# Attention in a two-layer backbone step: TensorE's program order pinned, modulation weights a page at a time, rows of maxima on SP's queue

## The chip, the cores and the metric

The kernel runs on one core of a Trainium2 chip. It is one launch that reads its inputs from the chip's memory and writes all outputs there. The metric is the device time of one execution in microseconds, the median of several. The engines in the profile are TensorE (PE, with its weight load PEld), VectorE (DVE), ScalarE (ACT), GpSimd (POOL) and SyncE (SP), and 16 DMA engines. DMAs are issued from two queues here: SP's (q1 in the profile) and ACT's (q10).

## The reference

Two layers over 128 context tokens and 1024 latent tokens, width 1024. In each layer a modulated norm feeds one input projection whose columns go to four groups: differential attention, multi-head latent attention (mla), grouped-query attention (gqa) and a Fourier mix. Their outputs go through one output projection, and an MLP follows. What matters here is the attention, which every head computes as

```python
def one_block(qb):
    logits = jnp.concatenate([jnp.einsum("bqhd,bkhd->bhqk", q_i, k_i)
                              for q_i, k_i in zip(qb, keys)], axis=-1) * scale
    probs = jax.nn.softmax(logits, axis=-1)
    ...   # out = sum over parts of einsum("bhqk,bkhd->bqhd", probs, v_i)
```

over the latent keys, the context keys and the cache of 128 past positions, and the modulation, which both token kinds take from

```python
mods = jax.nn.silu(c) @ w + b      # w is ada_w: (1024, 6 * 1024) for each layer
```

There are 16 softmax maps in a layer: eight for the four differential heads, four gqa, four mla.

## The kernel before

Everything is computed with channels or positions in the 128 partitions. Operands of matrix products are split into a high and a low half where the precision asks for it. In the code a layer goes through the norm and the input projection, then `attention`, then the output projection and the MLP. Pages of 4 KB in each partition (`pg` in the profile) are handed out and given back by the kernel itself: `t` takes one, `free` returns it, and a load into a page waits until the last user of that page is done.

`attention` runs over the 16 maps i of a layer (0 to 7 differential, one pass of scores each; 8 to 11 gqa, two passes; 12 to 15 mla, three passes). For map i it interleaves four generators with `run`, which always steps the one that is furthest behind its share:

- `stav(Ms[i])`: scores and products with V of map i, in ten pieces of up to 1024 columns. Scores go into `psB` (TensorE), ACT takes exp from it (L1340) and copies it to 16 bits (L1347), POOL subtracts to get the low half (`sub`, L287), and then TensorE multiplies both halves with V into `psC`. Between a piece's scores and its products with V lie `LAG` pieces, which `pend` holds and `settle` lets go.
- `beside(i)`: first `begin` issues the loads of map i+2 (`stack_diff`, `stack_gqa`, `stack_mla`: queries `qr` and `qp`, keys `kk`). For differential and mla maps `kk` is a tile of 97 rows by 1152 columns, loaded from `sk` or `mk` in one DMA. Then it takes `smax` of map i+1 to its end and some steps (`SMX`) of map i+2. `smax` computes the maxima of each query's scores ahead of the map: products into `psA`, `reduce_max` on DVE (L1297, L1302) into `mx` and `mm`, a small product that turns the nine columns into rows, a scaling into `mr` (L1311), and two DMAs of 4.0 and 4.5 KB that write `mr` into one more row of the query tiles `qr` and `qp` of that map, from where the score products subtract them. At step `LATE` the second and third parts of gqa and mla maps are loaded.
- `mods(MODS[l][i])`: steps of `mod_tiles`, the modulation. One tile has four pages of `ada_w` (`in_ada_p`, 512 KB each, loaded by `mod_stage`), eight products with `csil` (`mod_mm`), a copy on ACT (`acopy`, L290) and four small products with `quads`.
- `values(VM[i])`: V of the mla maps.

Deferred steps (`defer`, `tick`) finish a map: `epi_norm` and its like on DVE, a transposition on TensorE (L1441), and a store of the result to `y_dram` on ACT's queue.

The order in which an engine runs its instructions is not the order of the code. Before, a scheduler chooses among the instructions of all generators by priority (`pri`, `SC_PRI`), and the DMAs on SP's queue are put in an order by it too. An engine runs its own list strictly in order, and so does a queue: an instruction that waits holds everything behind it. A DMA signals its completion on one of eight semaphores that are taken in turn, so an issue may also wait for an older DMA that used the same one.

Lines of the profile: L271 is a DMA issued on SP (`dma`), L275 one on ACT (`dma2`), L278 a product on TensorE (`mm`), L287 a subtraction (`sub`), L290 a copy on ACT (`acopy`).

Of the kernel before, what the change touches and what calls it, by code (L numbers as in the profile page):

```python
# [52 lines left out]
MODS = ((0, 2, 2, 2, 2, 2, 2, 2, 2, 2, 2, 2, 2, 2, 2, 2), (0, 2, 2, 2, 2, 2, 2, 2, 2, 2, 0, 0, 0, 0, 0, 0))  # L53
# [11 lines left out]
LAG = (5, 5, 5)  # L65
LATE = 7
# [4 lines left out]
YO_PRI, RE_PRI, SC_PRI = 40, 60, (60, 0, 0)  # L71
# [129 lines left out]
class Kern:  # L201
    def __init__(self, ctx, tc, I, O):
        self.tc, self.nc, self.I, self.O = tc, tc.nc, I, O
        self.const = ctx.enter_context(tc.tile_pool(name="const", bufs=1))
        sl = ctx.enter_context(tc.tile_pool(name="slots", bufs=1))
        self.small = ctx.enter_context(tc.tile_pool(name="small", bufs=4))
        self.psA = ctx.enter_context(tc.tile_pool(name="psA", bufs=2, space=PSUM))
        self.phase = ctx.enter_context(ExitStack())
        self.split_now = None
        dram = ctx.enter_context(tc.tile_pool(name="dram", bufs=1, space=DRAM))  # L210
        self.sb = Arena(sl, NPG)
        self.x_dram = dram.tile([D, NT], F32, name="x_dram")
        self.y_dram = dram.tile([KT, 128, NT], F32, name="y_dram")
        self.spill(dram)
        self.n = 0
        self.cnt = 0
        self.nx = 0
        self.todo = deque()
        self.pend = deque()
        self.late = []  # L220
        self.ready = set()
        self.ylast = {}
        self.acc = {}
        self.wqk = []

# [51 lines left out]
    def mm(self, out, lhsT, rhs, start, stop, skip=False):  # L277
        self.nc.tensor.matmul(out, lhsT=lhsT, rhs=rhs, start=start, stop=stop, skip_group_check=skip)  # L278
# [144 lines left out]
    def mod_tiles(self, l, js):  # L423

        todo = [(j, half) for j in js for half in range(2)]
        w = self.mod_stage(l, *todo[0])
        yield
        for i, (j, half) in enumerate(todo):
# [4 lines left out]
            if i + 1 < len(todo):  # L433
                w = self.mod_stage(l, *todo[i + 1])
# [11 lines left out]
            yield  # L446

# [5 lines left out]
    def mod_stage(self, l, j, half):  # L453
        return [self.stage(self.I["ada_p"][l, 2 * j + half, g], [128, 2, 512]) for g in range(4)]
# [828 lines left out]
    def smax(self, M):  # L1283
# [23 lines left out]
        nc.vector.reduce_max(mm[:, 0:8], mx, axis=AX.X)  # L1307
        p = self.ps("A")
# [4 lines left out]
        for q, n in M["mrow"][1:]:  # L1313
            self.dma2(q.f[row:row + 1, 0:128 * n].rearrange("o (t c) -> o t c", t=n), mr[0:n, :].bitcast(F32))
        yield

    def stav(self, M):
# [33 lines left out]
        def av(pieces, pp):  # L1351

            for x, (b, c) in enumerate(pieces):
# [15 lines left out]
                if end:  # L1369
                    self.defer(D_EP, lambda b=b, o=o: epi(b, o))  # L1370
            self.free(pp)
# [4 lines left out]
        for pieces in [*(pair(0, c) for c in (0, 2, 4, 6)), [(0, 8), (1, 8)],  # L1376
                       *(pair(1, c) for c in (0, 2, 4, 6)), [(2, 9)]]:
            with self.pri(SC_PRI[M["kind"]]):
                self.pend.append((av, pieces, scores(pieces)))
            self.tick()  # L1380
            yield
            self.settle(LAG[M["kind"]])
            yield
# [18 lines left out]
    def settle(self, n):  # L1402

        while len(self.pend) > n:
            f, *a = self.pend.popleft()
            f(*a)
# [29 lines left out]
    def y_move(self, src, k, b, g):  # L1436
# [3 lines left out]
        for j in range(self.nj(b)):  # L1440
            nc.tensor.transpose(pt[:, 128 * j:128 * j + 128], src[:, j, :], self.ident)  # L1441
# [72 lines left out]
    def attention(self, l, st, Ms, side, out):  # L1514


        nm = len(MAPS)

# [9 lines left out]
        def beside(i):  # L1528
            if i + 2 < nm:
                self.begin(l, i + 2, st, Ms)  # L1530
            yield from steps(i + 1, 26)
# [12 lines left out]
        for i in range(nm):  # L1544
            n = 0
            if i + 1 < nm:
                n += 25 - Ms[i + 1]["done"]
            if i + 2 < nm:
                n += SMX[MAPS[i] // 4]
            run((self.stav(Ms[i]), 20), (beside(i), max(n, 1)), (mods(MODS[l][i]), MODS[l][i] + 1),  # L1550
# [3 lines left out]
        self.settle(0)  # L1554
# [481 lines left out]
    def leading(self, l, st, Ms):  # L2036

        for i, n in ((0, 26), (1, LEAD)):
# [145 lines left out]
```

## Time and profile before

| what | value |
|---|---|
| median of 3 runs | 3569.08 us (3566.26 to 3570.95) |
| the profiled execution's own time | 3559.4 us |
| its span in the trace | 3557.6 us |
| mean granted clock of TensorE | 0.933 of full speed |
| TensorE busy | 3197.4 us, 90% of the span |
| VectorE, ScalarE, GpSimd busy | 65%, 40%, 42% |
| attention of layer 0, 366.0 to 905.6 us | 539.6 us |
| attention of layer 1, 2134.0 to 2605.3 us | 471.3 us |

The bounds of attention are cut at the first exp of each map (line 1340, the first that reads `psB`); the same cut gives the maps within it. Each map has ten of these. In the differential maps of layer 0 the cuts are at 366.0, 393.6, 433.4, 469.3, 507.2, 541.6, 576.4 and 610.0 us; in layer 1 at 2134.0, 2161.9, 2195.7, 2223.2, 2254.1, 2283.5, 2313.9 and 2347.5. The gqa maps begin at 641.6 and 2384.0, the mla maps at 785.4 and 2499.7.

In a row of the timeline the engine, the line, the operation, what it writes and reads, and how many like it follow; in brackets the idle time of the engine before it and what ended it. An engine name with a q (SPq, ACTq) is a DMA issue on that engine's queue.

### The profile page before, as it was taken

The numbers are of one execution on the slowest core, as the hardware profiler recorded it, in microseconds if no ns is written. First come the engines' busy times: TensorE is split into PE (matmuls) and PEld (weight loads), VectorE is DVE, ScalarE is ACT, GpSimd is POOL, SyncE is SP. The second block draws the span as 40 slices with busy tenths as digits, with TensorE's granted clock in tenths as the row PEclk, the third lists the DMA queues.
The fourth block names the chain that finished last, engine by engine and source line by source line (L and its number), as shares of the span: only waits on it lengthen the run. The fifth ranks groups of instructions, "written<-read, shape, count | busy, mean of one in ns | idle before, by whom it ended". The sixth has DMA issues, their size and how long they took to land. (4 is left out here: it accounts for less than half of the span.)

```text
span 3557.6 us, 59006 instructions
## 1 busy us (share of the span) xinstructions
PE 3197.4 (90%) x23242; PEld 2580.5 (73%) x23242; DVE 2314.7 (65%) x4851; ACT 1424.4 (40%) x2290; POOL 1477.1 (42%) x1146
## 2 busy tenths in 40 slices
PE   7897878978898999999989978889989899999998
PEld 5886656757886777777779866667788677777776
DVE  6765535545368777777687665545545877777776
ACT  4332545645363222222243326656735322222222
POOL 1331465855554222222253216668745522222232
PEclk8998788889999999999999988889999999999998
DMA  5643323442301111111036434433330111111111
GB/s 213 201 144 94 120 84 116 130 124 89 124 32 57 36 48 46 44 42 48 30 105 210 148 103 122 130 94 94 102 130 30 48 48 37 48 48 36 48 36 54
DMA packets 140544, 310.81 MB, mean 87 GB/s; under 512 B 16613, under 2 KB 85682, under 8 KB 140266
## 3 DMA queue, kind: packets, MB, share of 16 engines
q1 hardware_dynamic: 134858, 300.85, 26.2%
q10 hardware_dynamic: 5408, 6.18, 0.5%
q8 instruction: 183, 3.00, 0.4%
q14 instruction: 95, 0.78, 0.1%
HBM read 233.87 MB, written 72.82 MB: 86 GB/s over the span
## 5 line engine op out<-in xcount | busy, mean ns | idle before, releaser
L278 PE MATMUL psD<-pg,pg 128*128 128x384 f32 (+4 forms) x11170 | 2101.9, 347 | 112.4 <-DVE pg L1769 45.5
L287 POOL TENSOR_TENSOR pg<-pg,pg 128x1024 f16<-128x1024 f32 (+8 forms) x741 | 1209.4, 1648 | 1140.2 <-ACT pg L290 581.4
L278 PEld LDWEIGHTS psD<-pg,pg 128*128 128x128 f32 x8184 | 1427.4, 193 | 73.4 <-DVE pg L287 18.7
L278 PEld LDWEIGHTS <-pg 128*128 128x128 f16 x11448 | 644.3, 102 | 487.2 <-issue 148.7
L1640 DVE SCALAR_TENSOR_TENSOR pg<-psD,mods,pg 128x256 f32<-128x256 f32 (+1 forms) x1088 | 520.5, 511 | 222.8 <-PE psD L278 220.1
L290 ACT ACTIVATE pg<-pg 128x512 f16<-128x512 f32 (+8 forms) x557 | 326.0, 617 | 742.9 <-PE psD L278 345.1
L278 PE MATMUL psA<-pg,pg 128*128 128x128 f16 (+7 forms) x2731 | 495.3, 297 | 119.1 <-DMA pg<-sk 35.4
L287 DVE TENSOR_TENSOR pg<-pg,pg 128x512 fp32r<-128x512 f32 (+12 forms) x605 | 469.8, 794 | 72.0 <-ACT pg L290 56.2
L1340 ACT ACTIVATE pg<-psB 128x1024 f32<-128x1024 f32 x320 | 298.5, 947 | 299.0 <-PE psB L278 263.3
L1297 DVE TENSOR_REDUCE mx<-psA 128x1 f32<-128x384 f32 x512 | 279.4, 554 | 197.6 <-PE psA L278 189.5
L278 PEld LDWEIGHTS psA<-pg,pg 96*128 96x128 f32 (+2 forms) x1377 | 254.1, 210 | 190.5 <-issue 64.7
L278 PE MATMUL psC<-pg,pg 128*128 128x65 f16 (+1 forms) x7008 | 346.5, 203 | 8.2 <-POOL pg L287 7.9
L278 PE MATMUL psB<-pg,pg 97*128 97x512 f32 (+3 forms) x1064 | 336.4, 431 | 2.1 <-ACT pg L1340 1.4
L1347 ACT ACTIVATE pg<-pg 128x1024 f16<-128x1024 f32 (+1 forms) x320 | 302.6, 979 | 23.5 <-POOL pg L287 7.6
L278 PEld LDWEIGHTS psB<-pg,pg 97*128 97x128 f32 (+3 forms) x1064 | 198.3, 205 | 40.2 <-issue 9.4
L1302 DVE TENSOR_REDUCE mx<-psA 128x1 f32<-128x384 f32 x256 | 141.9, 554 | 131.0 <-PE psA L278 126.4
L1669 POOL PARTITION_ALL_REDUCE wm<-wm x32 | 12.4, 387 | 373.1 <-DVE wm L1668 287.1
L1731 DVE TENSOR_TENSOR pg<-pg 128x512 f32<-128x512 f32 (+2 forms) x192 | 125.2, 666 | 52.1 <-ACT pg L1730 49.0
L1727 ACT ACTIVATE pg<-pg,wm 128x512 f32<-128x512 f32 x90 | 64.9, 722 | 207.8 <-DVE pg L1778 112.4
L513 ACT ACTIVATE pg<-pg 128x384 f32<-128x384 f32 x120 | 61.2, 522 | 144.3 <-DVE pg L1640 130.1
L1682 ACT ACTIVATE pg<-pg,wm 128x1024 f32<-128x1024 f32 x32 | 36.9, 1154 | 201.5 <-DVE wm L1938 201.4
L1695 POOL TENSOR_TENSOR pg<-pg 128x512 f32<-128x512 f32 x32 | 44.8, 1399 | 163.1 <-PE psD L278 148.7
(182 smaller groups left out, 1910.7 us busy)
## 6 DMA issues: line engine op xcount, KB each, us to landing
pg<-in_mlp_w SPq DMA_DIRECT2D x128, 512.0 KB
pg<-in_ada_p SPq DMA_DIRECT2D x96, 512.0 KB
pg<-in_w_out SPq DMA_DIRECT2D x16, 512.0 KB
pg<-y_dram SPq DMA_DIRECT2D x42, 192.0 KB
pg<-sk SPq DMA_DIRECT2D x16, 436.5 KB
sqp<-pg SPq DMA_DIRECT2D x36, 192.0 KB
mqp<-pg SPq DMA_DIRECT2D x36, 192.0 KB
pg<-sqp SPq DMA_DIRECT2D x16, 432.0 KB
```

Source lines behind the costliest of these rows:

```text
L278: self.nc.tensor.matmul(out, lhsT=lhsT, rhs=rhs, start=start, stop=stop, skip_group_check=skip)
L287: eng.tensor_tensor(out, a, b, ALU.subtract)
L290: self.nc.scalar.activation(out, in_, AF.Copy)
L513: self.nc.scalar.activation(q.t, x, AF.Square)
L1297: nc.vector.reduce_max(mx[:, t, i:i + 1], p[:, 0:TB], axis=AX.X)
L1302: nc.vector.reduce_max(mx[:, t, 2:3], p[:, 128:512], axis=AX.X)
L1340: nc.scalar.activation(e[:, 0:n], src, AF.Exp, scale=M["scale"])
L1347: nc.scalar.activation(pp[:, 0, 0:n], e[:, 0:n], AF.Copy)
L1640: self.nc.vector.scalar_tensor_tensor(xs, o(p), self.mods[:, l, 8 * j + m, s:s + 1], xs, op0=ALU.mult, op1=ALU.add)
L1695: nc.gpsimd.tensor_tensor(s1.t, a21, a22, ALU.add)
L1727: nc.scalar.activation(r.t, src, AF.Relu, scale=W[c][1])
L1731: nc.vector.tensor_tensor(r.t, r.t, r.t, ALU.mult)
```

## The change

- Within `attention` every TensorE instruction that goes through `mm`, and the transpositions of `y_move`, is now kept in program order among its like (`pin`, with the flag `pinned`). What the code writes first, TensorE runs first. The priority of scores (`SC_PRI`) is dropped.
- So that the program order is finer, the generators yield more often: the products with V of one piece yield between their two halves (`settle` and `av` are generators now), `smax` yields once more before its last product (27 steps, `N_MX`, were 26), and `mod_stage` yields after each page. The step counts that `run` shares by follow (20 to 29 for `stav`, `MODS` from 2 to 6 steps for a tile).
- `mod_tiles` issues the next tile's pages after the small products of this tile, one page a step, where it issued all four at once between a tile's large and small products.
- `LAG` goes from 5 to 4 pieces, `LATE` from step 7 to step 5.
- The two DMAs of `mr` are issued on SP's queue (`dma`), not on ACT's (`dma2`).

```diff
-MODS = ((0, 2, 2, 2, 2, 2, 2, 2, 2, 2, 2, 2, 2, 2, 2, 2), (0, 2, 2, 2, 2, 2, 2, 2, 2, 2, 0, 0, 0, 0, 0, 0))
+MODS = ((0, 6, 6, 6, 6, 6, 6, 6, 6, 6, 0, 2, 4, 4, 6, 6), (0, 6, 6, 6, 6, 6, 6, 6, 6, 0, 0, 0, 0, 0, 0, 0))
-LAG = (5, 5, 5)
-LATE = 7
+LAG = (4, 4, 4)
+N_MX = 27
+LATE = 5
-YO_PRI, RE_PRI, SC_PRI = 40, 60, (60, 0, 0)
+YO_PRI, RE_PRI = 40, 60
...
     def mm(self, out, lhsT, rhs, start, stop, skip=False):
-        self.nc.tensor.matmul(out, lhsT=lhsT, rhs=rhs, start=start, stop=stop, skip_group_check=skip)
+        self.pin(self.nc.tensor.matmul(out, lhsT=lhsT, rhs=rhs, start=start, stop=stop, skip_group_check=skip))
+
+    def pin(self, ins):
+
+        if self.pinned:
+            self.tc.keep_in_program_order(ins)
...
     def mod_tiles(self, l, js):
-        w = self.mod_stage(l, *todo[0])
-        yield
+        w = []
+        yield from self.mod_stage(l, *todo[0], w)
         for i, (j, half) in enumerate(todo):
...
-            if i + 1 < len(todo):
-                w = self.mod_stage(l, *todo[i + 1])
+            w = []
             r = self.t([128, 512])
             self.acopy(r.t, acc)
             yield
...
             yield
+            if i + 1 < len(todo):
+                yield from self.mod_stage(l, *todo[i + 1], w)
...
-    def mod_stage(self, l, j, half):
-        return [self.stage(self.I["ada_p"][l, 2 * j + half, g], [128, 2, 512]) for g in range(4)]
+    def mod_stage(self, l, j, half, w):
+        for g in range(4):
+            w.append(self.stage(self.I["ada_p"][l, 2 * j + half, g], [128, 2, 512]))
+            yield
...
         nc.vector.reduce_max(mm[:, 0:8], mx, axis=AX.X)
+        yield
         p = self.ps("A")
...
-            self.dma2(q.f[row:row + 1, 0:128 * n].rearrange("o (t c) -> o t c", t=n), mr[0:n, :].bitcast(F32))
+            self.dma(q.f[row:row + 1, 0:128 * n].rearrange("o (t c) -> o t c", t=n), mr[0:n, :].bitcast(F32))
...
                     self.defer(D_EP, lambda b=b, o=o: epi(b, o))
+                if x + 1 < len(pieces):
+                    yield
...
-            with self.pri(SC_PRI[M["kind"]]):
-                self.pend.append((av, pieces, scores(pieces)))
+            self.pend.append((av, pieces, scores(pieces)))
             self.tick()
             yield
-            self.settle(LAG[M["kind"]])
+            yield from self.settle(LAG[M["kind"]])
...
-            run((self.stav(Ms[i]), 20), (beside(i), max(n, 1)), (mods(MODS[l][i]), MODS[l][i] + 1),
+            run((self.stav(Ms[i]), 29), (beside(i), max(n, 1)), (mods(MODS[l][i]), MODS[l][i] + 1),
```

Three places in the order, before and after. The numbers behind a name count the tile and its use; they tell rows apart and mean nothing across the two kernels.

TensorE before, in an early differential map of layer 0: products with V (`psC`), one piece's scores (`psB`), products with V again, products of maxima (`psA`).

```order
L278 MATMUL psC_388_3841<-pg28_196_3198,pg35_252_3736 128x65
L278 MATMUL psB_401_3964<-pg14_209_3258,pg21_211_3260 128x512 x2
L278 LDWEIGHTS pg35_252_3736
...
L278 MATMUL psA_403_3999<-pg33_238_3551,pg32_237_3550 128x256
L278 MATMUL psA_403_3999<-pg33_238_3551,pg30_236_3549 128x256
L278 MATMUL psA_405_4011<-pg17_173_2372,pg32_237_3550 128x128
L278 LDWEIGHTS pg15_254_3778
L278 MATMUL psC_388_3841<-pg25_197_3199,pg15_254_3778 128x65
```

Here the scores stand in the midst of one piece's products with V (ten rows ahead of them and six behind read the same weights), and the products of maxima stand where their operands were first to be had.

TensorE after, at a like place:

```order
L280 MATMUL psC_382_3818<-pg29_193_2980,pg26_248_3660 128x64
L280 MATMUL psA_389_3876<-pg33_238_3551,pg30_236_3549 128x384
L280 MATMUL psA_390_3879<-pg33_238_3551,pg30_236_3549 128x384
L280 MATMUL psA_391_3882<-pg33_238_3551,pg32_237_3550 128x256
L280 MATMUL psA_391_3882<-pg33_238_3551,pg30_236_3549 128x256
L280 MATMUL psA_392_3886<-pg33_238_3551,pg30_236_3549 128x384
L280 MATMUL psB_393_3889<-pg18_210_3267,pg23_212_3269 128x512 x2
L280 MATMUL psA_394_3904<-pg33_238_3551,pg30_236_3549 128x384
L280 LDWEIGHTS pg37_250_3706
L280 MATMUL psC_382_3818<-pg9_195_3197,pg37_250_3706 128x65
```

The products with V of one half piece are done, then come products of maxima, the scores of one piece, one more product of maxima, and the next half piece's products with V, as the generators yield.

SP before, the DMAs of one early map of layer 0 (`sqr`, `sqp`: queries, `sk`: the 97-row load, `in_ada_p`: pages of a modulation tile):

```order
L271 DMA pg24_291_4316<-sqp1_74 96x1152
L271 DMA pg35_302_4477<-in_ada_p 128x1024
L271 DMA pg18_299_4471<-in_ada_p 128x1024
L271 DMA pg41_290_4315<-sqr1_73 96x1024
L271 DMA pg3_292_4317<-sk1_76 97x1152
L271 DMA pg21_300_4473<-in_ada_p 128x1024
L271 DMA pg0_301_4475<-in_ada_p 128x1024
```

Two pages stand ahead of the 97-row load and two behind it; the rows of maxima are on ACT's queue and do not appear.

SP after, the same map and the rows of maxima around it:

```order
L273 DMA pg30_236_3549<-mr_408_4042 1x8x128
L273 DMA pg32_237_3550<-mr_408_4042 1x9x128
L273 DMA pg3_286_4338<-sqr1_73 96x1024
L273 DMA pg40_288_4340<-sk1_76 97x1152
L273 DMA pg6_287_4339<-sqp1_74 96x1152
L273 DMA pg24_289_4348<-in_ada_p 128x1024
L273 DMA pg0_292_4404<-in_ada_p 128x1024
L273 DMA pg21_300_4531<-in_ada_p 128x1024
L273 DMA pg15_295_4464<-in_ada_p 128x1024
L273 DMA pg20_259_3897<-mr_457_4490 1x8x128
L273 DMA pg10_260_3898<-mr_457_4490 1x9x128
```

The three loads of a map come first, then the four pages of a tile, then the two transfers of the next map's maxima. In map 0 the order is another:

```order
L273 DMA pg31_261_3899<-sk0_75 97x1152
L273 DMA pg20_259_3897<-sqr0_71 96x1024
L273 DMA pg18_210_3267<-mr_367_3698 1x8x128
L273 DMA pg21_211_3268<-mr_367_3698 1x9x128
L273 DMA pg10_260_3898<-sqp0_72 96x1152
```

There the two transfers of maxima come right behind a 97-row load and its first queries.

## Rows read from the trace of the kernel before

**Rows 1.** Stretches: bounds, length, busy PE PEld DVE ACT POOL (count), clock, DMA share, GB/s.

```profile
366.00:905.60 539.60, 451.77 (x4829) 338.84 (x4829) 261.69 (x607) 308.31 (x357) 331.29 (x224) 0.85 0.37 110
2134.00:2605.30 471.30, 428.89 (x4734) 324.72 (x4733) 261.60 (x595) 304.70 (x354) 330.85 (x224) 0.90 0.36 108
```

**Rows 2.** TensorE's waits in layer 0's attention: total us, times, longest us.

```profile
PE psA L278 <- DMA pg<-sk: 29.9, 4, 9.6
PE psA L278 <- ACT pg L290: 16.8, 1, 16.8
...
PE psA L278 <- DMA pg<-in_ada_p: 9.2, 2, 7.4
```

**Rows 3.** Timeline of SP's queue, 428 to 460 us: start, length, issue.

```profile
429.04 0.24 SPq L271 DMA_DIRECT2D pg<-sk  x1
429.34 10.31 SPq L271 DMA_DIRECT2D pg<-in_ada_p  x2
```

**Rows 4.** Timeline of all engines, 440 to 460 us.

```profile
447.22 0.70 ACTq L275 DMA_DIRECT2D pg<-mr  x1
...
453.35 0.66 PE L278 MATMUL psA<-pg,pg 96*128 96x384 f32 x1 [5.99 <-DMA pg<-sk]
```

**Rows 5.** DMA view, 443 to 452 us: queue, packets, MB, share.

```profile
q1 hardware_dynamic: 51, 0.24, 6.3%
```

**Rows 6.** DMA view, 448 to 449 us, ACT's queue.

```profile
q10 hardware_dynamic: 14, 0.00, 1.6%
```

**Rows 7.** DMA view, 450 to 452 us, ACT's queue.

```profile
q10 hardware_dynamic: 2, 0.00, 0.1%
```

**Rows 8.** DMA view, 452.65 to 455.6 us, SP's queue.

```profile
q1 hardware_dynamic: 17, 0.06, 5.1%
```

**Rows 9.** TensorE's waits in layer 1's attention.

```profile
PE psA L278 <- DMA pg<-mqr: 3.7, 1, 3.7
...
PE psA L278 <- DMA pg<-mk: 3.4, 1, 3.4
PE psA L278 <- DMA pg<-sk: 3.1, 2, 2.1
```

**Rows 10.** Busy time by groups of maps, columns as in rows 1.

```profile
393.60:576.40 182.80, 139.61 (x1477) 97.48 (x1477) 78.41 (x198) 93.26 (x109) 103.95 (x74) 0.82 0.35 105
2195.70:2313.90 118.20, 106.20 (x1186) 76.17 (x1185) 64.87 (x162) 74.84 (x87) 84.39 (x63) 0.89 0.44 128
2161.90:2195.70 33.80, 27.30 (x294) 17.05 (x293) 15.24 (x38) 18.56 (x22) 19.69 (x12) 0.89 0.37 121
576.40:641.60 65.20, 60.05 (x561) 40.90 (x561) 35.16 (x92) 37.20 (x42) 38.95 (x24) 0.79 0.33 98
2313.90:2384.00 70.10, 64.84 (x615) 43.95 (x615) 38.15 (x104) 37.40 (x42) 40.53 (x25) 0.80 0.31 95
...
2527.10:2553.10 26.00, 26.00 (x314) 21.63 (x313) 14.69 (x33) 18.85 (x20) 19.27 (x11) 1.00 0.17 48
785.40:905.60 120.20, 109.50 (x1282) 88.28 (x1281) 62.12 (x122) 78.72 (x89) 76.72 (x39) 0.96 0.35 104
2499.70:2605.30 105.60, 99.69 (x1213) 82.41 (x1211) 62.41 (x112) 77.56 (x86) 74.83 (x39) 0.98 0.34 98
...
641.60:785.40 143.80, 115.51 (x1285) 90.89 (x1284) 68.75 (x160) 81.45 (x99) 92.92 (x82) 0.85 0.43 126
2384.00:2499.70 115.70, 103.78 (x1205) 83.95 (x1203) 63.16 (x144) 78.55 (x97) 92.72 (x81) 0.94 0.33 94
```

**Rows 11.** Timeline of all engines, 722 to 760 us, in gqa map 10.

```profile
752.22 0.28 ACT L290 ACTIVATE pg<-psA 128x128 f32<-128x128 f32 x1 [21.42 <-DMA pg<-mk]
...
752.55 0.80 PE L278 MATMUL psA<-pg,pg 96*128 96x256 f32 x2 [16.81 <-ACT pg L290]
```

**Rows 12.** The chain that ended last, 2090 to 2610 us: start, length, what.

```profile
2437.82 20.08 DMA pg<-mk
```

**Rows 13.** Groups of POOL by shape, 366 to 905 us: count, busy us, mean ns.

```profile
L287 POOL TENSOR_TENSOR pg<-pg,pg 128x1024 f16<-128x1024 f32 x142 | 301.9, 2141 | 186.2 <-ACT pg L1347 125.2 <-PE psB L278 21.9 <-PE psC L278 17.2
```

More of the change, by code (lines that the diff above doesn't have):

```diff
@@ L224, in __init__ @@
         self.wqk = []
+        self.pinned = False
     def pri(self, n):
@@ L1405, in settle @@
             f, *a = self.pend.popleft()
-            f(*a)
+            yield from f(*a)
     def values(self, o, n):
@@ L1440, in y_move @@
         for j in range(self.nj(b)):
-            nc.tensor.transpose(pt[:, 128 * j:128 * j + 128], src[:, j, :], self.ident)
+            self.pin(nc.tensor.transpose(pt[:, 128 * j:128 * j + 128], src[:, j, :], self.ident))
         self.free(src)
@@ L1517, in attention @@
         nm = len(MAPS)
+        self.pinned = True
         def steps(i, n):
@@ L1530, in beside @@
                 self.begin(l, i + 2, st, Ms)
-            yield from steps(i + 1, 26)
+            yield from steps(i + 1, N_MX)
             yield from steps(i + 2, SMX[MAPS[i] // 4])
@@ L1546, in attention @@
             if i + 1 < nm:
-                n += 25 - Ms[i + 1]["done"]
+                n += N_MX - Ms[i + 1]["done"]
             if i + 2 < nm:
                 n += SMX[MAPS[i] // 4]
-            run((self.stav(Ms[i]), 20), (beside(i), max(n, 1)), (mods(MODS[l][i]), MODS[l][i] + 1),
+            run((self.stav(Ms[i]), 29), (beside(i), max(n, 1)), (mods(MODS[l][i]), MODS[l][i] + 1),
                 (values(VM[i]), VM[i] + 1), (out if i == nm - 1 else iter(()), 14))
@@ L1553, in attention @@
                 self.free(*st["vd" if i == 8 else "vg"])
-        self.settle(0)
+        for _ in self.settle(0):
+            pass
+        self.pinned = False
         while self.late:
@@ L2036, in leading @@
     def leading(self, l, st, Ms):
-        for i, n in ((0, 26), (1, LEAD)):
+        for i, n in ((0, N_MX), (1, LEAD)):
             self.begin(l, i, st, Ms)
```

## The prediction

> **What bounds the kernel now.** I read the times of whole stretches first, then the waits of TensorE inside them, then the queue that those waits lead to. Outside attention the instruction order of every engine stays practically the same, so the question is what happens in two stretches: the 16 attention maps of layer 0 and of layer 1, 539.6 and 471.3 us [rows 1]. The work is the same in both, 4829 and 4734 TensorE instructions, and yet layer 0 takes 68.3 us more. In neither is TensorE busy all the time, and its granted clock averages 0.85 and 0.90 of 2.4 GHz. A stretch that takes 15% longer with the same work is bound by waits. The list of TensorE's waits in layer 0 names three: 29.9 us in four waits for `pg<-sk`, 16.8 us in one for ACT, 9.2 us in two for `in_ada_p` pages [rows 2].
>
> The first is a load of keys. SP issues it at 429.04 and issues two modulation pages right behind it [rows 3]; TensorE's next product starts at 453.35, after 5.99 us of waiting for it [rows 4], so issue to use is 24.3 us. Why a load of 437 KB takes that long is in the DMA view: while it is alone, SP's queue q1 moves 51 packets in 9 us [rows 5], 178 ns each, one after another. The load has 97 rows, of which each is a packet or so; 97 x 178 ns = 17.3 us on what looks like a single DMA engine. The eight-row transfer of maxima, issued at 447.22 on ACT's queue [rows 4], has 14 packets moved at once [rows 6], and two more only after 450 [rows 7], while the long load is still running. And the pages that SP issued behind the load have their last 17 packets moved alone, after it [rows 8]. So: a load on q1 waits for the 97 rows with the part of itself that goes to their engine, and a transfer on q10 waits a few us at most.
>
> So a map takes as long as this load unless TensorE has enough other work between its issue and its use. In layer 1 the waits on it are 3.1 us in two [rows 9], and four maps take 118.2 us [rows 10], 29.55 each; in layer 0 five such maps take 182.8, 36.6 each. Behind every stall the clock falls to half: 0.82 against 0.89 in the same rows. In the order of before, layer 0 has its load issued later against TensorE's program than layer 1; that is the whole difference I can see between them.
>
> The 16.8 us are another story: in map 10 ACT stands still for 21.42 us because its queue is at a store of `y_dram`, which waits for the landing of an `mk` load; TensorE waits for ACT's next result [rows 11].
>
> **The change part by part**, against the profiled execution's own 3559.4 us (its span is 3557.6); the median of the runs shown is 3569.08, 9.7 more, and I add that at the end.
>
> *Program order on TensorE, one yield per part, LAG 4.* Nothing is added to TensorE's work. What moves is where page frees fall and so where SP can issue. In the order of after, both layers issue the 97-row load of map i+2 in the middle of map i-1 and use it in map i, with the same distance in both, about that of layer 1 before. I therefore give layer 0 the pace of layer 1: five maps from 182.8 to 5 x 29.55 = 147.8, **-35.0**; the one map of layer 1 still outside it, from 33.8 [rows 10] to 29.55, **-4.3**. The four maps of layer 1 at that pace stay as they are: **0**, because the load still sets their period. Maps 6 and 7 load no 97 rows; 65.2 and 70.1 us for the four of both layers. They have a floor of 26.0 us, which a map took with TensorE busy throughout at clock 1.00 [rows 10], and the pace of 29.55 as the upper end; the middle, 27.8, makes 4 x 27.8 = 111.2, **-24.1** (bounds -17 and -31).
>
> *The store in map 10.* In after, stores of `y_dram` no longer share a completion semaphore with a long load that is just issued: the gqa stretch of layer 0, 143.8 us, comes down to that of layer 1, 115.7 [rows 10], **-28.1**. In layer 1 the waits for `mk` 3.4 and `mqr` 3.7 [rows 9] go with LATE = 5, which brings the late loads two tiles earlier: **-7.1**. A load of that kind takes 20.08 us [rows 12], and by the order some 20 us of TensorE's work (an estimate) then stand between its issue and its use.
>
> *mla maps.* 120.2 us in layer 0, 105.6 in layer 1 [rows 10]. The difference of 14.6 holds modulation tiles that layer 0 still has there, before and after. I take a third, **-5** (bounds 0 and -14.6).
>
> *Modulation a page at a time.* The same 96 pages and products. ACT and DVE do the same. The four pages of a tile are issued in successive steps right after the long load, where before two of four stood ahead of it. Each page brings a few packets behind the 97 rows on their engine, so TensorE may wait for a tile as it does now, 9.2 us in two waits: taken as **0** (bounds -9 and +10). What would hide it is the work between the last page and its product, by the order 8 us and more (an estimate); without it each of the 20 tiles in attention could cost what the longest such wait does, 7.4 us.
>
> *POOL and LAG.* One piece's low half takes 2.14 us on POOL [rows 13], ten pieces some 20 us of a 29.55 us map. Four pieces of lag are 4 x 2.96 = 11.8 us between scores and products with V, against 2.14 us on POOL and some 2 on ACT: the cover holds, **0**. If POOL is behind by three pieces it doesn't; that is within the range.
>
> *The maxima on SP's queue.* ACT loses the 62 issues of attention, 0.7 us each beside its stream [rows 4], where they cost nothing now. On SP the two transfers stand in line with everything that SP issues: they wait for DVE's `mr`, and the loads of map i+2 and the pages behind them wait for that. Where a 97-row load was issued just ahead, one row of the transfer comes behind it. In the order this is so in map 0 of both layers, in map 12 of layer 0 and at two mla maps of layer 1: five places. In the diff maps between, the order issues the row when the load ahead of it is nearly due itself. The price of one: bounds 0 and 17.3; the nearest rows are the waits on the very same load, 29.9/4 = 7.5 us in layer 0 [rows 2] and 3.1/2 = 1.6 in layer 1 [rows 9]. I take the middle, 4.5: 5 x 4.5 = **+22** (bounds 0 and 87).
>
> On this the Trainium skill, page "DMA: Bandwidth & Descriptors", section "Queues, rings and completion order", speaks against the change: SP and ACT each own one ring on each of the same 16 engines, an engine takes turns between rings, and within a ring it consumes descriptors in order. The trace agrees with it in 14 packets at once and two a little later on q10, and in the pages' 17 late packets on q1. The same page's "Issuing engines are not separate DMA queues" says that issuing from several engines saves only the sequencer's time; by it the term would be 0 and the sum 22 us lower. The first has the rows on its side.
>
> Sum: -35.0 - 4.3 - 24.1 - 28.1 - 7.1 - 5 + 22 = -81.6; 3559.4 - 81.6 = 3477.8, and with 9.7 the median is **3487**.
>
> **Rivals.**
>
> *A, more gain (18%).* The regular order keeps TensorE from stalling, so the clock stays up and the load is covered everywhere: diff maps 1 to 7 at 26.0 us. Layers: 182.8 + 65.2 to 182.0, -66.0; 33.8 + 118.2 + 70.1 to 182.0, -40.1; gqa -35.2; mla -14.6; maxima 0. That is -155.9, or 3413. For it: a map at 26.0 exists. Against: the load's 24.3 us leave next to nothing.
>
> *B, little gain (18%).* The load is issued when pages come free, and pages come free as late as before: half of -35.0 in layer 0 and nothing in maps 6 and 7 or mla; the store goes. -17.5 - 35.2 + 22 = -30.7, or 3538. For it: SP waits for pages now, not for TensorE's order as such.
>
> *C, nothing (6%).* The pinned order takes away the freedom by which the scheduler filled stalls with other products, and gives back what the store brings: 3562 to 3576.
>
> *D, slower (14%).* The row of maxima waits behind the 97 rows in every map that has such a load ahead of it, ten in a layer, twenty in all. A row issued at any moment of 17.3 us waits 8.65 on average: 20 x 8.65 = +173, against -103.6 from the other terms: +69.4, or 3639. It decides from 103.6/20 = 5.2 us a map. The section on rings says that the row does wait whenever the load is in flight. For it: [rows 8]. Against: in the order the row comes late in the load's flight, since the load is issued half a map earlier.
>
> **How the numbers follow.** The forecast has 44%, by itself 3440 to 3525; A 18, B 18, C 6, D 14. A measurement of this kernel tells about 0.2% (7 us) from no change. Faster is the forecast, A and B: 0.80; same C: 0.06; slower D: 0.14. The range leaves out D and a little of A: 3395 to 3575, which holds the ends of the terms (maps 6 and 7, mla, pages, maxima up to 70).
>
> **What would show it.** In the profile after: layer 0's attention near 460 us and layer 1's near 455; waits for `pg<-sk` in layer 0 under 10 us; no wait of TensorE for ACT above 3 us; the store's 21.42 us gone; waits for `pg<-mr`, absent now from TensorE's list, at the start of map 1 in both layers, together some 22 us; mean clock above 0.933. Wrong would be: `pg<-sk` still at 30 us with diff maps of layer 0 at 36 us (B); `pg<-mr` with 60 us or more, or products of scores starting late in every map (D); scores waiting for POOL or ACT, which says that LAG 4 is too short; or any stretch outside attention that moves by more than 5 us.

## The result, and the profile after

The changed kernel takes 3522.69 us (median, 3521.58 to 3528.47) against 3569.89 of before: a ratio of 0.9873, 95% interval 0.9856 to 0.9890. It is 47 us faster where 82 were forecast, inside the range of 3395 to 3575. The profiled execution took 3522.5 us, its span is 3520.6, 37.0 us shorter than that of before; TensorE's mean clock is 0.944 in place of 0.933.

Where the 37 us lie is read from the busy time by stretch of the changed kernel, cut at the first exp of a map as before. Columns: bounds, length, busy time of PE, PEld, DVE, ACT and POOL with their counts, clock, DMA share, GB/s. The rows are the two attentions; then, layer 0 and layer 1 in turn, maps 1 to 5, 6 and 7, gqa, mla; last map 0 of each layer.

```profile
365.60:856.00 490.40, 418.08 (x4849) 320.48 (x4848) 272.44 (x609) 316.04 (x358) 335.38 (x225) 0.91 0.41 123
2075.60:2566.80 491.20, 417.54 (x4757) 322.89 (x4757) 268.98 (x596) 314.15 (x354) 336.06 (x225) 0.88 0.35 103
...
400.50:544.80 144.30, 124.37 (x1490) 90.47 (x1489) 86.65 (x205) 97.42 (x108) 106.07 (x74) 0.89 0.40 123
2096.10:2254.30 158.20, 130.20 (x1491) 92.50 (x1491) 86.51 (x206) 97.45 (x108) 108.16 (x76) 0.86 0.41 127
544.80:603.60 58.80, 47.92 (x600) 36.41 (x599) 36.44 (x92) 38.52 (x43) 39.51 (x22) 0.91 0.38 119
2254.30:2316.50 62.20, 51.01 (x599) 37.70 (x599) 36.28 (x91) 38.48 (x43) 39.49 (x22) 0.84 0.35 106
603.60:718.20 114.60, 105.77 (x1265) 85.98 (x1265) 65.93 (x155) 82.68 (x99) 92.13 (x82) 0.99 0.47 132
2316.50:2445.00 128.50, 106.89 (x1240) 87.81 (x1240) 65.60 (x153) 82.18 (x97) 92.03 (x82) 0.91 0.35 96
718.20:856.00 137.80, 119.46 (x1298) 91.93 (x1296) 67.31 (x124) 79.97 (x89) 78.35 (x39) 0.90 0.40 115
2445.00:2566.80 121.80, 109.80 (x1230) 89.48 (x1230) 64.57 (x113) 78.47 (x87) 79.16 (x38) 0.92 0.28 81
...
365.60:400.50 34.90, 20.57 (x204) 15.69 (x203) 16.10 (x34) 17.46 (x21) 19.32 (x10) 0.74 0.42 134
2075.60:2096.10 20.50, 19.64 (x207) 15.40 (x207) 16.02 (x34) 17.57 (x21) 17.23 (x9) 0.90 0.31 89
```

Layer 0's attention is 49.2 us shorter than in [rows 1], layer 1's 19.9 us longer; the rest of the kernel gives 7.7. So the two layers, which were 68 us apart, are now alike, and layer 1 has paid for part of it.

TensorE's waits in the changed kernel (total us, times, longest), layer 0's attention:

```profile
PE psB L280 <- DMA pg<-mr: 21.6, 3, 13.2
PE psA L280 <- DMA pg<-in_ada_p: 8.9, 6, 3.4
...
PE psA L280 <- DMA pg<-sk: 8.0, 3, 4.4
PE psC L280 <- POOL pg L294: 6.7, 2, 6.2
```

and layer 1's:

```profile
PE psB L280 <- DMA pg<-mr: 19.2, 3, 13.1
...
PE psA L280 <- DMA pg<-sqr: 8.1, 3, 4.1
PE psA L280 <- DMA pg<-sk: 7.3, 1, 7.3
```

Against [rows 2] the 29.9 us for `pg<-sk` are 8.0 and the 16.8 us for ACT are gone. In their place stand 40.8 us for `pg<-mr`, which before had no line at all: 13.2 us in map 0 of layer 0, 7.2 in map 12, 13.1 in map 27 and 4.8 in map 28, and two of about 1 us. One of them in full. SP's queue first:

```profile
375.73 0.24 SPq L273 DMA_DIRECT2D pg<-sk  x1
377.33 3.28 SPq L273 DMA_DIRECT2D pg<-sqr  x1
380.70 2.13 SPq L273 DMA_DIRECT2D pg<-mr  x2
382.94 0.40 SPq L273 DMA_DIRECT2D pg<-sqp  x1
```

then TensorE, which begins the scores of map 1:

```profile
399.23 1.19 PE L280 MATMUL psB<-pg,pg 97*128 97x512 f32 x2 [13.16 <-DMA pg<-mr]
```

and what the DMA engines moved from 388 to 399 us, in 40 equal slices:

```profile
DMA  9962915889641100000000000000000000000008
GB/s 374 344 255 76 257 32 227 287 344 419 225 168 45 32 34 17 34 17 34 34 17 34 17 34 17 34 34 17 34 17 34 17 34 34 15 30 30 17 35 61
```

The maxima are issued 5 us after the 97-row load. From about 391.5 us on everything else has been moved and 17 to 34 GB/s are left, the rows of that load one by one, as in [rows 5]. One row of each transfer of the maxima comes when they end: the trace has two packets of 512 bytes at 398.45 and 398.48, right behind the load's last. Two transfers of 4 KB have taken 16 to 18 us, and TensorE stood still for 13 of them.

The gain in layer 0's differential maps shows in SP's queue:

```profile
413.48 0.24 SPq L273 DMA_DIRECT2D pg<-sk  x1
...
442.29 0.24 SPq L273 DMA_DIRECT2D pg<-sk  x1
...
471.00 0.24 SPq L273 DMA_DIRECT2D pg<-sk  x1
...
499.70 0.25 SPq L273 DMA_DIRECT2D pg<-sk  x1
```

The loads are 28.7 us apart, and the maps take 28.9 on average. Before, they were issued at 429.04, 466.73, 504.60 and 539.13: 36.7 apart on average.

### The profile page after: what moved, and what is told of

It reads as the page before. It is cut to its first block, busy times and chain, and to the rows that moved or that the text cites. A ratio compares the mean times of both kernels' runs of the same rounds, so it can differ in the third digit from the quotient of the medians.

```text
span 3520.6 us, 59002 instructions
## 1 busy us (share of the span) xinstructions
PE 3140.4 (89%) x23242; PEld 2552.8 (73%) x23242; DVE 2333.3 (66%) x4851; ACT 1442.1 (41%) x2290; POOL 1486.7 (42%) x1146
## 4 chain that ended last, share of the span: by engine, by line
PE 47%; DVE 14%; DMA 13%; issue 11%; POOL 7%; ACT 3%; SPq 1%; POOLq 0%; DVEq 0%; ACTq 0%
PE psD L280 30%; PE psA L280 8%; POOL pg L294 6%; PE psB L280 5%; DVE pg L294 4%; PE psC L280 3%; DMA pg<-sk 2%; DMA pg<-mr 2%; DMA pg<-in_ada_p 2%; DVE pg L1655 2%; DMA pg<-mqp 1%; DMA pg<-sqr 1%; ACT pg L297 1%; SPq L273 1%; DVE pg L1746 1%
## 5 line engine op out<-in xcount | busy, mean ns | idle before, releaser
L294 POOL TENSOR_TENSOR pg<-pg,pg 128x1024 f16<-128x1024 f32 (+7 forms) x738 | 1216.0, 1663 | 1201.4 <-ACT pg L297 542.4
L280 PEld LDWEIGHTS <-pg 128*128 128x128 f16 x11448 | 632.3, 101 | 469.0 <-issue 126.0
L280 PE MATMUL psA<-pg,pg 128*128 128x128 f16 (+6 forms) x2757 | 497.1, 292 | 92.2 <-DVE mx L1307 19.5
L294 DVE TENSOR_TENSOR pg<-pg,pg 128x384 fp32r<-128x384 f32 (+9 forms) x594 | 472.5, 814 | 62.1 <-ACT pg L297 40.8
L280 PE MATMUL psB<-pg,pg 97*128 97x512 f32 (+3 forms) x1064 | 328.8, 425 | 44.2 <-DMA pg<-mr 40.8
L280 PE MATMUL psC<-pg,pg 128*128 128x65 f16 (+1 forms) x7008 | 332.9, 200 | 14.0 <-POOL pg L294 13.5
L1358 ACT ACTIVATE pg<-pg 128x1024 f16<-128x1024 f32 x320 | 311.6, 982 | 24.2 <-POOL pg L294 5.7
L1312 DVE TENSOR_REDUCE mx<-psA 128x1 f32<-128x384 f32 x256 | 142.0, 555 | 80.8 <-PE psA L280 67.7
L811 POOL TENSOR_TENSOR pg<-pg,pg 128x384 f32<-128x384 f32 (+1 forms) x54 | 57.1, 1062 | 111.1 <-ACT pg L297 24.9
```

What stands on the lines that cost most here:

```text
L280: self.pin(self.nc.tensor.matmul(out, lhsT=lhsT, rhs=rhs, start=start, stop=stop, skip_group_check=skip))
L294: eng.tensor_tensor(out, a, b, ALU.subtract)
L811: nc.gpsimd.tensor_tensor(t2.t, s[:, 0:w], tab[0][:, c], ALU.mult)
L1312: nc.vector.reduce_max(mx[:, t, 2:3], p[:, 128:512], axis=AX.X)
L1358: nc.scalar.activation(pp[:, 0, 0:n], e[:, 0:n], AF.Copy)
```

## The experiments

The theory to be tested had two parts: (1) 97 rows on one DMA engine set the pace, and what is queued behind them on SP waits; (2) the pinned program order is what moves the load ahead in layer 0. Their rivals: that the waits only show at these places and go elsewhere when moved, and that another part of the change moves the load. Kernels are compared by their ratio to the kernel before, timed on the same chip; the changed kernel has 0.9873, and 0.001 is 3.6 us. Two parts of the change are tested in no run by themselves: the finer yields, and the priority of scores that it drops.

**The maxima back on ACT's queue.**

```diff
-            self.dma(q.f[row:row + 1, 0:128 * n]...
+            self.dma2(q.f[row:row + 1, 0:128 * n]...
```

> The changed kernel, with the two transfers of maxima back on ACT's queue; nothing else. Theory (the row of maxima that belongs to the DMA engine of a 97-row load waits behind that load on SP's queue): the 40.8 us that TensorE waits for pg<-mr in both layers go, and the half clock behind them: 3522.7 goes to 3465 to 3485, attention of layer 1 from 491 to some 465 us, no wait for pg<-mr above 2 us. Rival (the place is late for another reason, and the wait only shows there): the wait goes over to pg<-sk, pg<-mk or DVE at the same maps, and the time stays within 3510 to 3530.

3494.33 us, 0.9815 (0.9794 to 0.9837): some 21 us faster than the changed kernel. The waits for `pg<-mr` are gone but for 2.5 us, so part (1) holds. The gain is less than expected, in part because a new wait stands in map 12. The timeline there:

```profile
744.38 0.75 ACTq L277 DMA_DIRECT2D pg<-mr  x1
...
759.89 0.33 ACTq L277 DMA_DIRECT2D y_dram<-pg  x1
760.27 1.94 ACT L1351 ACTIVATE pg<-psB 128x1024 f32<-128x1024 f32 x2 [15.61 <-DMA pg<-mk]
...
761.35 2.93 PE L280 MATMUL psB<-pg,pg 97*128 97x512 f32 x6 [11.68 <-ACT pg L1351]
```

This is the stall of [rows 11] again: a store on ACT's queue waits for the landing of a 97-row `mk` load, issued at 737.44. In the trace both have the same completion semaphore, number 101. With the maxima on ACT's queue the eight semaphores are dealt otherwise, and a store again draws the one that a load holds. So it depends on the number and order of DMAs before it whether that stall is there.

**The 97-row load in two, in the changed kernel.**

```diff
     def load(self, tile_, p, src):
+        if p == 97 and src.shape[-1] == NT:
+            self.dma(tile_.f[0:96, 0:NT], src[0:96])
+            self.dma(tile_.f[96:97, 0:NT], src[96:97])
+            return
         self.dma(tile_.f[0:p, 0:src.shape[-1]], src)
```

> The changed kernel, with each load of a 97-row key tile issued as two: 96 rows, then the one that is left; the same bytes. Theory (97 rows go one after another on one DMA engine, and this sets the pace of the differential maps and the waits for pg<-mr): issue to landing falls from over 20 us to under 8; waits for pg<-mr, pg<-sk, pg<-mk and pg<-mqr go, differential maps come to 20 to 27 us from 28 to 36, and the time to 3390 to 3440. Rival (the load is slow for its bytes or for what is moved at the same time): it still takes 15 us or more, and the time stays above 3500.

3359.15 us, 0.9433 (0.9406 to 0.9461): 157 us off the changed kernel, more than expected. SP's queue and the DMA view from 401 to 412 us:

```profile
401.16 0.66 SPq L273 DMA_DIRECT2D pg<-sk  x2
401.86 0.31 SPq L273 DMA_DIRECT2D pg<-sqp  x1
402.27 10.56 SPq L273 DMA_DIRECT2D pg<-in_ada_p  x4
```

```profile
GB/s 119 268 253 268 290 253 130 201 235 285 302 201 201 218 235 149 132 264 192 242 207 125 263 257 238 238 313 417 417 387 402 328 179 104 15 15 0 15 15 15
```

The same bytes, with the queries and two pages beside them, are moved by 410 us, mostly at 200 GB/s and more; the trickle at the end is a few packets. The trace has the last 4.6 KB row of the load and of `sqp` at 407.5, 6.4 us after the issue. TensorE's list in layer 0 is headed by DVE now, and neither `sk` nor `mk` is on it; of `mr` one wait of 1.3 us is left:

```profile
PE psA L280 <- DVE mx L1311: 11.4, 14, 2.3
...
PE psC L280 <- POOL pg L294: 8.4, 3, 7.6
```

Attention falls to 437.4 and 426.5 us. And it is not attention alone: the stretch between the two attentions loses another 21 us and the one ahead of the first 22. TensorE waits 10.7 us less for ACT between the attentions, and ahead of the first its wait of 3.3 us for `sk` is gone. ACT itself had stood still there in the changed kernel, before 365.6 us:

```profile
ACT pg L297 <- DMA mqr<-pg: 12.9, 1, 12.9
...
ACT pg L297 <- DMA pg<-in_dft_lat: 8.5, 1, 8.5
```

The first of these ends at 278.5, and the transfers that it names stand on SP's queue behind a 97-row load issued at 258.60. With the split the first is 3.8 us and the second isn't listed; between the attentions these are 14.8 and 16.4 us, and with the split neither is listed. The split therefore also helps where no map is computed. How much of the 22 and 21 us comes this way was not tested.

**The same split in the kernel before.**

> The kernel before, with the same split of the 97-row loads. Theory: its waits for pg<-sk (29.9 us in layer 0) and for pg<-mk go and with them the half clock behind them, and ACT's stall of 21.4 us at the store in map 10: 3569.9 goes to 3460 to 3510. If it comes as low as the changed kernel with the split (within 10 us), then the changed order is worth nothing but better cover for this load. Rival (the scheduler's order itself costs the time, by its mixing of scores and products with V): 3540 or more.

3412.43 us, 0.9589 (0.9570 to 0.9608). This one edit takes 147 us off the kernel before, three times what the whole change did. It is also better than either theory had it. With the split on both sides the change is still worth 0.0156, some 55 us. So it isn't only better cover for this load, which is what the prediction mostly had it down for. In the two profiles layer 0's attention is 454.4 against 437.4, layer 1's 451.6 against 426.5; layer 1's differential maps 1 to 5 (142.0 against 128.0) and 6 and 7 (70.7 against 59.8) show it most. It isn't TensorE's waits that shrink here: its busy time in the two attentions falls from 849.7 to 794.1 us, at a granted clock of 0.95 in both where it was 0.93 and 0.90. Two runs below keep this gain without the pin (0.9387) and with the maxima on ACT's queue (0.9461), so neither of these parts is needed for it. Which part brings it stays open.

**The pin taken away.**

```diff
-        self.pinned = True
+        self.pinned = False
```

> The changed kernel with the pin taken away: the scheduler chooses TensorE's order again, from the same code with its finer yields, one lag less, late loads two tiles earlier and the maxima on SP's queue. Theory (the pinned order moves the issue of the 97-row load ahead against TensorE's program): layer 0's waits for pg<-sk come back, 3540 to 3570. Rival (finer yields, LAG and LATE do it, the pin is only a form): 3515 to 3530.

3512.99 us, 0.9867 (0.9841 to 0.9894), as with the pin. Layer 0's maps 1 to 5 take 152.6 us in place of 144.3, still far from the 182.8 of [rows 10], and the mla maps are shorter, 130.8 for 137.8. Part (2) of the theory is out: the pin accounts for 8 us of the 38.5 at most. Without the 97-row load in the way it looks no better:

> The changed kernel with the 97-row loads split and without the pin. Theory (the pin is worth nothing by itself: without the split it was 0.987 of before with it and 0.987 without): the same as the split with the pin within 12 us, 0.940 to 0.947 of before. Rival (while the load binds, the order is hidden behind it; with the load gone the regular order shows): 15 us or more slower than with the pin, 0.948 or more, towards the 0.959 of the kernel before with the split.

3344.34 us, 0.9387 (0.9352 to 0.9422), a little faster than the split with the pin (0.9433), though the intervals overlap. The mla maps, where TensorE has most work, show it in both layers: 109.9 and 104.0 us without the pin, 117.9 and 110.9 with it. That a scheduler free to choose finds other work there fits with it, but was not looked at further.

**The modulation as before, in the changed kernel** (both functions and `MODS` put back).

> The changed kernel with the modulation as it was before (all four pages of a tile issued in one step, right behind the large products; the old step counts), everything else as changed. Theory now (with the pin out of the question, it is the place of the pages on SP's queue that decides when the 97-row load is issued: two pages ahead of it before, none after): layer 0's issues of that load go back from 28.8 us apart to 34 and more, waits for pg<-sk in layer 0 to 25 us or more, 3545 to 3575. Rival (one lag less or the earlier late loads do it): within 8 us of the changed kernel, 3515 to 3530.

3539.24 us, 0.9934 (0.9911 to 0.9957): 22 us slower than the changed kernel, somewhat less than the theory had it, and not for its reason. Layer 0's maps 1 to 5 are shorter still, 136.9 us, with the loads 28.6 us apart. What is slower is elsewhere: gqa in layer 0, 155.4 for 114.6, with waits for `pg<-mr` of 14.5 and 13.4 us in maps 10 and 11. So in the changed kernel the place of the pages does not decide when the load is issued.

**The modulation a page at a time alone, in the kernel before.**

> The kernel before with only the modulation taken a page at a time, with its step counts. Theory (any change that takes the two pages from ahead of the 97-row load gives layer 0 the pace of layer 1): layer 0's differential maps 1 to 5 come from 182.8 to some 150 us, waits for pg<-sk under 15 us, 3525 to 3550. Rival (only the maxima on SP's queue, or the finer yields, set the load earlier): within 8 us of before.

3495.43 us, 0.9802 (0.9772 to 0.9832): 71 us faster than before, 25 us faster than the whole change. Layer 0's maps 1 to 5 take 164.5 us. SP's queue:

```profile
409.87 0.33 SPq L271 DMA_DIRECT2D pg<-sqr  x1
410.73 0.24 SPq L271 DMA_DIRECT2D pg<-sk  x1
411.07 4.74 SPq L271 DMA_DIRECT2D pg<-sqp  x1
415.90 6.84 SPq L271 DMA_DIRECT2D pg<-in_ada_p  x4
```

All four pages stand behind the load now (in the order shown ahead, two stood in front of it), and so does `sqp`, which was ahead of it too; it is issued at 410.73 where it was at 429.04 [rows 3]. TensorE's wait for it in layer 0 is 5.5 us for 29.9:

```profile
PE psA L278 <- DMA pg<-in_ada_p: 6.0, 1, 6.0
PE psA L278 <- DMA pg<-mk: 5.9, 1, 5.9
PE psA L278 <- DMA pg<-sk: 5.5, 2, 3.8
```

These maps are held back by the clock: it is granted at 0.75 on average, and TensorE is busy 147.9 us of 164.5.

```profile
392.80:557.30 164.50, 147.93 (x1487) 108.24 (x1486) 81.68 (x196) 93.72 (x109) 106.63 (x76) 0.75 0.35 106
```

So the load's earlier issue is not the whole gain. The profile is 62.8 us shorter than that of before: 18.4 in these maps, 25.3 in maps 6 to 11 of layer 0 (209.0 to 183.7), where ACT's 21.4 us stall is not there, and 17.5 between the two attentions, which no run explains.

**The maxima on SP's queue alone, in the kernel before.**

> The kernel before with only the two transfers of maxima moved to SP's queue. Theory (a row of them stands behind the 97-row load on one DMA engine): TensorE waits for pg<-mr in most maps whose next but one is differential or mla; 20 maps by 2 to 6 us, 3590 to 3680, slower; ACT's 21.4 us stall at the store of map 10 may move, as the completion semaphores are dealt otherwise. Rival (the place is free, as in the maps of the changed kernel whose transfer comes when the load is nearly done): within 10 us of before.

3558.38 us, 0.9966 (0.9951 to 0.9981), a little faster, against the theory. Layer 0's maps 1 to 5 come to 144.0 us here too, its load issued at 417.28, 447.29, 474.44 and 499.41: that edit also changes what SP's queue does first. The price is paid elsewhere: `pg<-mr` 16.6 and 12.6 us in maps 27 and 28, and ACT stands still at a store for 18.5 us in map 10 and 12.9 in map 12, of which TensorE waits 16.1 and 8.5. So the slow pace of layer 0 isn't undone by one part of the change. The pages' edit alone does half of it and the maxima's edit alone all of it; with the pin, the pages or the lag taken back most of it stays undone (152.6, 136.9 and 156.2 us).

**LAG 5.**

```diff
-LAG = (4, 4, 4)
+LAG = (5, 5, 5)
```

> The changed kernel with LAG 5 in place of 4. Theory (the modulation's pages decide): within 8 us of the changed kernel; POOL's 6 us wait in maps 7 and 23, which has to do with POOL's backlog, goes. Rival (a piece's page is given back one piece sooner and with it the page that the 97-row load waits for): layer 0's load is issued later, waits for pg<-sk above 20 us, 3540 or more.

> The changed kernel with the 97-row loads split and LAG 5. Theory (LAG 5 was 40 us faster without the split by chance: waits for the maxima fell on other maps, and the MLP of layer 1 was 29 us shorter): with the split within 12 us of LAG 4, 0.940 to 0.947. Rival (four pieces do not cover POOL, whose wait of 7 us is seen in maps 7 and 23 at LAG 4): these waits go and the time is 0.938 or less.

Without the split 3479.34 us, 0.9753 (0.9719 to 0.9787); with it 3315.66, 0.9302 (0.9275 to 0.9328), the fastest kernel here, 7% below before. So the changed kernel is 43 and 47 us faster with LAG 5. But only a part of that lies in attention: the two attentions together are 14.3 us shorter with LAG 5 in the one pair (layer 0's 14.8 longer, layer 1's 29.1 shorter), 9.9 in the other. The POOL waits of maps 7 and 23 do get shorter, without the split from 6.2 and 6.5 us to 2.0 and 5.9. The larger part is in the MLP of layer 1, behind both attentions, where `LAG` isn't used. With the split, LAG 5:

```profile
2388.90:3309.30 920.40, 863.53 (x5263) 699.12 (x5259) 667.79 (x1265) 283.72 (x508) 311.07 (x241) 0.98 0.15 52
```

and with the split, LAG 4:

```profile
2405.70:3356.60 950.90, 873.46 (x5240) 701.85 (x5236) 677.21 (x1265) 284.38 (x508) 305.69 (x241) 0.97 0.14 50
```

30.5 us between them for the same work. TensorE's waits in that stretch, LAG 5:

```profile
PE psD L280 <- DVE pg L1788: 10.7, 7, 2.0
```

and LAG 4:

```profile
PE psD L280 <- DVE pg L1788: 29.6, 13, 3.4
```

Some 19 us of it is the wait for one step on DVE. Among all kernels here this stretch takes either 920 to 925 us (these two with LAG 5, and the next kernel) or 947 to 957 (the eleven others). The traces say what the two lengths are: two orders of the same instructions. ScalarE's 508 of that stretch stand alike, but for one or two, in the three short kernels, and alike in the long ones, but some 100 stand elsewhere between the two kinds. LAG does not decide which it is: the kernel before and its three variants have LAG 5 and the long order, and the next kernel has LAG 4 and the short one. So of the 43 and 47 us some 30 go with that order, and 10 to 14 can be put down to the lag in attention. What in the code decides the order stays open.

**LATE 7.**

```diff
-LATE = 5
+LATE = 7
```

> The changed kernel with LATE 7 in place of 5 (the late loads of gqa and mla maps two tiles later, as before). Theory of the prediction (LATE 5 takes the waits for mk and mqr away, some 7 us): waits for these come back, 3525 to 3545. Rival (LATE 5 puts the long load of an mla map ahead of the maxima's transfer, which is what costs 13.1 and 4.8 us in maps 27 and 28): these waits for pg<-mr shrink, 3490 to 3515.

3516.64 us, 0.9864 (0.9829 to 0.9899): no difference, and neither side is right. The waits for `pg<-mr` grow, to 61.0 us in all. In the profile attention is 9.6 us longer, the stretch between the two attentions 14.3 longer, and the MLP of layer 1 32.4 shorter (921.5 us). So without the MLP's other order LATE 7 would have been some 24 us slower (an estimate, 9.6 and 14.3); the total hides it.

**The split, with the maxima on ACT's queue.**

> The changed kernel with the 97-row loads split in 96 rows and one, and the maxima on ACT's queue. Theory (with the load spread there is nothing left for the row to wait behind): the same as with the split alone within 10 us, 0.943 of before; the queue of the maxima is then worth nothing either way. Rival (the row still costs on SP's queue, behind 512 KB pages): 15 us or more faster than with the split alone.

3372.90 us, 0.9461 (0.9435 to 0.9488), against 0.9433 with the maxima on SP's: the same within the intervals. Once no load sits on a single DMA engine, the queue of the maxima makes no difference here.

## Why the prediction held, and where its steps failed

**What bounds the kernel: right, and larger than said.** The 97 rows on one DMA engine were read from three DMA rows; the split shows them to be worth 147 us in the kernel before. The prediction counted only the waits that name the load (30 us) and its pace. In the profiles of the kernel before, without and with the split, TensorE's idle time falls by 100 us and its busy time by 47, with the mean clock going from 0.933 to 0.954. By place, 85 and 20 us of it lie in the two attentions, and 25 ahead of them and 15 between them, where the prediction looked for nothing.

**Layer 0's maps 1 to 5: size right, cause wrong.** Forecast -35.0, measured -38.5 (182.8 to 144.3). The step said that program order on TensorE moves the load; with the pin off the maps stay at 152.6. What the runs show instead is the order on SP's queue. Before, three transfers stood ahead of each load: `sqp`, at which SP stood still for 17 to 22 us until a product with V was done, and two pages, for up to 7 us more. One such place:

```profile
420.38 0.33 SPq L271 DMA_DIRECT2D pg<-sqp  x1
426.59 1.88 SPq L271 DMA_DIRECT2D pg<-in_ada_p  x2
```

From 364 to 576 us SP's waits for products with V are 131.1 us in the kernel before and 25.7 in the changed one:

```profile
SPq L271 <- PE psC L278: 131.1, 13, 22.1
SPq L273 <- PE psC L280: 25.7, 7, 8.6
```

The pages' edit alone brings them to 30.0 us (the maps to 164.5) and the maxima's edit alone to 22.4 (144.0), and in both the load is issued earlier. No run moves `sqp` or the two pages alone, so their shares are not shown. The term that the prediction set at 0, a page at a time, is by itself worth 71 us in the kernel before and 22 in the changed one, though only 18 of the 71 lie in these maps.

**Layer 1's maps 1 to 5: wrong.** Forecast -4.3, measured +6.2 (152.0 to 158.2): the load's loop stays, as said, with 7.3 us of waits for it where there were 3.1, and waits for `sqr` (8.1 us) join it.

**Maps 6 and 7:** forecast -24.1, measured -14.3 (135.3 to 121.0), short of the lower bound of 17; a wait for POOL of 6 us in map 7 of each layer, which the LAG term had as covered.

**gqa:** layer 0 forecast -28.1, measured -29.2, through the stall that goes. The reason given fits the runs, a store that no longer shares a semaphore with a load; that this hangs on the number and order of DMAs, and so could have come out otherwise, was not said. Layer 1 forecast -7.1, measured +12.8, because of the maxima in map 27: with them on ACT's queue it takes 113.9 us for 128.5.

**mla: the sign was wrong.** Forecast -5, measured +17.6 and +16.2. Some 14 of it are waits for the maxima in maps 12, 14, 28 and 30. TensorE's busy time is 10 us longer in each layer, at a clock of 0.90 for 0.96 and 0.92 for 0.98. Layer 0's mla maps also have three modulation tiles where they had two, with 5.9 us of waits for pages, which the prediction took as unchanged. In the split pair the pin alone makes mla maps 7 to 8 us longer in each layer.

**The maxima on SP's queue: places right, price too low.** Four of the five places named are those that waited (map 0 of layer 0, map 12, two mla maps of layer 1); map 0 of layer 1 didn't. The price was taken as 4.5 us, the middle of waits on the load itself; it measured 13.2, 7.2, 13.1 and 4.8, together with two small ones 40.8 for a forecast 22. The rows chosen for the price were the wrong neighbours: that load is issued a map ahead of its use, and what is waited for is its end; the maxima are needed soon after they are issued, so TensorE waits for most of the load. With the maxima back on ACT's queue only 21 us come back, in part because the stall at a store returns.

**LAG at 0: wrong by 10 to 14 us,** the cost of four pieces in attention. The other 30 us of the two LAG runs go with the MLP's order and are no part of the change, which leaves that stretch as it was (952.3 us before, 953.8 after).

**The signs named.** `pg<-sk` in layer 0 under 10 us (8.0), the store's stall gone and the clock above 0.933 (0.944) came as said. The attentions are 490.4 and 491.2 us, not 460 and 455, and the stretch between them moved by 8.8 us (1228.4 to 1219.6), where 5 outside attention were to be a sign of being wrong.

So the gain in the sum came out too large by the terms of layer 1, mla and the maxima, and the sign and the range held because layer 0's two large terms were sized from rows of the other layer doing the same work. For maps 1 to 5 that is luck, as the cause given for the size was not the one at work. It was close as well: 3522.69 lies 2 us inside the forecast's own 3440 to 3525, and 15 from rival B's 3538. Rival D's mechanism was real, but at six places, not twenty. The page on DMA (the Trainium skill, "DMA: Bandwidth & Descriptors", section "Queues, rings and completion order": in order within a ring, in turn between rings) is borne out by the 13 us, which are gone with the maxima on ACT's queue. The section "Issuing engines are not separate DMA queues" of that page of the Trainium skill, by which the issuing engine saves only the time to issue, holds here only once the load is split (0.9433 and 0.9461). The same page of the Trainium skill, section "Why a DMA increments its semaphore by 16 and not by 1", has the reason for the split: the count of engines is the largest up to 16 that divides the slowest dimension on both sides, which for 97 is one and for 96 sixteen. The trace agrees: 51 rows one by one in 9 us against 200 GB/s and more.

## What to carry to other kernels

Look at how many engines a load is on before asking where it is queued: 97 rows moved as 96 and 1 were worth three times a rework of the order around them. When several edits of an order are made at once, take each alone: here one of them alone was worth more than all together, and one nothing. And split each difference by stretch: two thirds of the 45 us that LAG seemed to cost lay in a stretch that LAG doesn't touch. A stall at a store that hangs on which semaphore it draws can come back with any change in the number or order of DMAs.

## What the runs showed that was not expected

A 4 KB transfer took 16 to 18 us to land behind a load on the same queue and engine. A DMA issue can stand still for 15 to 21 us for a load on another queue, which it has nothing to do with, through the completion semaphore that both draw. And an edit in attention moved the MLP of the last layer between two orders of the same instructions, 30 us apart at about the same clock (0.98 and 0.97).
